# Strassen block products for the input projection of a gated hybrid block, with linear attention's operands kept in DRAM

## The chip, the cores and the metric

One core of one Trainium2 chip runs the whole kernel. The metric is the device time of one execution in microseconds (us). Its compute engines are TensorE (PE, with its weight loads as PEld), VectorE (DVE), ScalarE (ACT) and GpSimd (POOL); SyncE (SP) issues nearly all transfers. Each engine works through its own list of instructions in a fixed order.

## The reference, cut to what matters

One decoder block over 1024 tokens of width 1024, in float32:

```
u  = RMSNorm(h)
z  = u @ W_in                   # 1024 x 1024 @ 1024 x 4272
c_q, c_kv, k_rope, g_q, g_k, g_v, g_lr, g_og, gate_a, gate_b = split(z)
y_a = mla(c_q, c_kv, k_rope, ...) @ W_oA     # softmax attention, 8 heads
y_b = gla(g_q, g_k, g_v, g_lr, g_og, ...) @ W_oB   # gated linear attention, 4 heads, chunked scan
h  = h + (sigmoid(gate_a) * y_a + sigmoid(gate_b) * y_b) @ W_out
h  = h + SwiGLU(RMSNorm(h)); out = RMSNorm(h)
```

The widths of the split are 384, 256, 32, 256, 256, 512, 16, 512, 1024, 1024. `gla` gates each key channel by a decay that depends on the token (`g_lr`), normalises each head's output and multiplies it by `silu(g_og)`.

## The kernel before

Every float32 product is made of three TensorE passes (`mm3`, L122 to L127): each operand is split into a rounded high part and the rest (`hi`, `lo`), and hi*hi, hi*lo and lo*hi are summed in PSUM. `split` (L106) rounds on ScalarE and subtracts on GpSimd.

The kernel runs in stages, all in one function `block_kernel`.

- **Start.** Eight token tiles of x are normalised (`norm_in`), transposed (`transpose_in`) and split into `uh`, `ul`: features on partitions, for each half of 512 tokens 8 chunks of the contraction. The first projections start in between (`begin`).
- **Projection.** `proj` takes 128 columns of W_in, one half of the tokens and 8 chunks: 24 matmuls of 512 columns. `proj_tm` makes token-major results with 256 columns. Queries, keys, values and log gates of linear attention come first and stay in SBUF (`q_fm`, `k_fm`, `b_fm`, `v_tm`); `spill` computes the rest (latents, branch gates) and sends it to DRAM from two staging tiles (`stg`, tag `st`).
- **Linear attention** (L334 to L438). Four units (two token halves, two pairs of heads). The level part of a unit builds the 128 x 128 score blocks `A` by seven levels m = 64 to 1: E = exp of decay differences (DVE L362, ACT L363 and L364), X = E*k (POOL L366), a block-diagonal query `qbd` = E*q (two DVE operations L373), four matmuls (L377) and a masked copy into `A` (DVE L379). The state part goes through four token tiles: output and state update on TensorE (L407 to L414), state (DVE L422, L424), sum of squares (ACT L431), reciprocal root (L87 on DVE, L88 on POOL) and scaling (DVE L437).
- Then the rest of the gates, the latents' norms and up-projections, the softmax attention (scores `pss` from L690), the merge, and a feed-forward part, which uses Strassen products already (`wpair`, `wsums`, `prod`).

The tile scheduler (`schedule_with_timeline_sim=True`) fixes each engine's list when the program is built: it goes by the order of the code, by free tiles and by its own model of time. The engine lists are therefore the same in each run.

Of the kernel before, what the change touches and what calls it, by code (L numbers as in the profile page):

```python
# [10 lines left out]
F32 = mybir.dt.float32  # L11
# [9 lines left out]
P = 128  # L21
# [22 lines left out]
ZFIRST = {29: 0, 31: 1}  # L44

@with_exitstack
def block_kernel(ctx, tc, x, positions, ln_mix, w_in, norm_cq, w_uq, norm_ckv, w_ukv, w_oa,
# [18 lines left out]
    d_c = dram.tile([704, S], F32, name="d_c")  # L66
    d_ob = dram.tile([512, S], F32, name="d_ob")
# [31 lines left out]
    def wraw(n):  # L99
        return wpool.tile([P, D], F32, name="wr", tag="wr", bufs=3)[:, :n]  # L100
# [29 lines left out]
    stg = pool("stg", bufs=2, side="left")  # L130
# [4 lines left out]
    upool = pool("upool", side="left", c=pux)  # L135

# [3 lines left out]
    uh, ul = [], []  # L140
    for h in range(2):
        us = [uslot(h).rearrange("p (e n) -> p e n", e=2) for c in range(KC)]
        uh.append([u[:, 0, :] for u in us])
        ul.append([u[:, 1, :] for u in us])
# [6 lines left out]

    win = w_in[0]

    def proj(hi, lo, half, M=P):
        ps = bank("mm")
        for c in range(KC):
            mm3(ps[:M], hi[:, c, :], lo[:, c, :], uh[half][c], ul[half][c], c == 0, c == KC - 1)
        return ps

    with ExitStack() as s1:  # L160
        xpool = pool("xpool", side="right", c=s1)

        def load_x(t):
            xt = xpool.tile([P, D], F32, name="xt", tag="xt", bufs=4)
            nc.sync.dma_start(xt, x2[t * P:(t + 1) * P, :])
            return xt

        def norm_in(xt):
            ssq = small.tile([P, 1], F32, name="ssq", tag="ssq")
            xs = xpool.tile([P, D], F32, name="xn", tag="xn", bufs=5)  # L170
            nc.scalar.activation(xs, xt, AF.Square, accum_out=ssq)
            r = small.tile([P, 1], F32, name="rx", tag="rx")
            rstd_of(r, ssq, 1, 1.0 / D, small)
            nc.vector.tensor_scalar(xs, xt, r, None, ALU.mult)
            return xs

        def transpose_in(xn, half):
            for c in range(KC):
                ps = bank("mm" if c < 4 and half == 0 else "g")
                for i in range(4):  # L180
                    nc.tensor.transpose(ps[:, i * P:(i + 1) * P], xn[i][:, c * P:(c + 1) * P], ident)
                gc = g_mix[:, c:c + 1]
                nc.scalar.activation(uh[half][c], ps, AF.Copy, scale=gc)
                nc.vector.scalar_tensor_tensor(ul[half][c], ps, gc, uh[half][c].bitcast(F32), ALU.mult,  # L184
                                               ALU.subtract)


        first = []

        def begin(off):  # L190
            w = wload(win[:, off:off + P], KC, P)
            first.append((w, proj(*w, 0)))

        transpose_in([norm_in(load_x(t)) for t in range(4)], 0)
        begin(O_GQ)
        begin(O_GQ + P)
        xn = [norm_in(load_x(t)) for t in range(4, 8)]
        begin(O_GK)
        transpose_in(xn, 1)
        begin(O_GK + P)  # L200
# [17 lines left out]
    wg2 = g.tile([P, HALF], F32, name="wg2", tag="kdT", bufs=1)[0:32, 0:256]  # L218
    nc.sync.dma_start(wg2[0:16, :], w_gate2[0])
    nc.sync.dma_start(wg2[16:17, :], b_gate)  # L220

    def proj_tm(w, t, n=256):
        ps = bank("mm")
        h, o = divmod(t, 4)
        for c in range(KC):
            ts = slice(o * P, (o + 1) * P)
            mm3(ps[:, :n], uh[h][c][:, ts], ul[h][c][:, ts], w[c][0], w[c][1], c == 0, c == KC - 1)
        return ps

    q_fm, k_fm, b_fm = ([[g.tile([P, HALF], F32, name=f"{nm}{p}{h}") for h in range(2)] for p in range(2)]  # L230
                        for nm in ("gq", "gk", "gb"))
    for off, dst, sc in ((O_GQ, q_fm, 0.125), (O_GK, k_fm, 1.0)):
        for p in range(2):
            w, ps = first.pop(0)
            for half in range(2):
                if half:
                    ps = proj(*w, half)
                nc.scalar.activation(dst[p][half], ps, AF.Copy, scale=sc)  # L238


    raw, hi, lo = wtiles(KC * 80)
    v3 = lambda t: t.rearrange("p (c n) -> p c n", c=KC)
    nc.sync.dma_start(v3(raw)[:, :, 0:16], win[:, O_LR:O_LR + 16].rearrange("(c p) n -> p c n", p=P))
    nc.sync.dma_start(v3(raw)[:, :, 16:48], win[:, O_KR:O_KR + 32].rearrange("(c p) n -> p c n", p=P))
    for (a, b) in ((0, 16), (32, 64)):
        o = 0 if a == 0 else 16
        nc.scalar.copy(v3(hi)[:, :, a:b], v3(raw)[:, :, o:o + b - a])
    nc.scalar.copy(v3(hi)[:, :, 64:80], v3(raw)[:, :, 32:48])
    nc.scalar.copy(v3(hi)[:, :, 16:32], v3(raw)[:, :, 16:32])
    for (a, b, o) in ((0, 16, 0), (32, 64, 16), (64, 80, 32), (16, 32, 16)):  # L250
        nc.vector.tensor_tensor(v3(lo)[:, :, a:b], v3(raw)[:, :, o:o + b - a], v3(hi)[:, :, a:b].bitcast(F32),
                                ALU.subtract)
    hi, lo = v3(hi), v3(lo)
    glr = g.tile([32, S], F32, name="glr", tag="A", bufs=2)
    nc.gpsimd.memset(glr, 1.0)
    for half in range(2):
        ps = proj(hi, lo, half, M=80)
        hs = slice(half * HALF, (half + 1) * HALF)
        nc.vector.tensor_copy(glr[0:16, hs], ps[0:16])
        st = stg.tile([P, HALF], F32, name="st", tag="st")  # L260
        nc.scalar.copy(st[0:80], ps[0:80])
        nc.sync.dma_start(d_c[640:672, hs], st[32:64])
        nc.sync.dma_start(d_c[672:688, hs], st[64:80])
        nc.sync.dma_start(d_c[688:704, hs], st[32:48])
# [33 lines left out]
    v_tm = [g.tile([P, 512], F32, name=f"v{t}") for t in range(NT)]  # L298
    for p in range(2):
        w = wload2(win[:, O_GV + p * 256:O_GV + (p + 1) * 256], 256)  # L300
        for t in range(NT):
            ps = proj_tm(w, t)
            nc.any.tensor_copy(v_tm[t][:, p * 256:(p + 1) * 256], ps[:, :256])


    la = []
    for i in range(4):
        ps = bank("g")
        for j in range(2):
            t = 2 * i + j  # L310
            nc.tensor.matmul(ps[:, j * 256:(j + 1) * 256], glr[0:17, t * P:(t + 1) * P], wg2[0:17, :],
                             start=True, stop=True)
# [3 lines left out]
        l = g.tile([P, HALF], F32, name="la", tag="on", bufs=8)  # L316
# [4 lines left out]
    for half in range(2):  # L321
        for p in range(2):
# [6 lines left out]
            nc.vector.tensor_copy(b_fm[p][half], ps)  # L329
# [11 lines left out]
    on = [None] * NT  # L341
    nq = 0
    state = [0, 0]
    for half in range(2):
        for p in range(2):
            q, k, b = q_fm[p][half], k_fm[p][half], b_fm[p][half]
# [51 lines left out]
            kdT = g.tile([P, HALF], F32, name="kdT", tag="kdT", bufs=1)  # L398
            nc.scalar.copy(kdT, psT)
            for i in range(4):  # L400
# [7 lines left out]
                for hd in range(2):  # L408
                    nc.tensor.matmul(po[:, hd * P:(hd + 1) * P], A[:, i * 2 + hd, :],
                                     v_tm[t][:, p * 256 + hd * P:p * 256 + (hd + 1) * P],  # L410
# [15 lines left out]
                if p == 0:  # L426
                    on[t] = g.tile([P, 512], F32, name="on", tag="on", bufs=8)
# [912 lines left out]
```

## Time and profile before

| | us |
|---|---|
| runs | 1539.46, 1539.59, 1542.38 (median 1539.59) |
| profiled execution | 1542.38, span of its instructions 1540.6 |
| PE busy / DVE / ACT / POOL | 1495.2 / 879.6 / 618.2 / 543.1 |
| mean granted TensorE clock | 0.993 of full speed |

The busy time of TensorE is modelled from pipelined matmuls, so 97% busy does not say that it issues at its full rate; the distance from one matmul's start to the next does. `ps_mm` and `ps_g` are the two sets of four PSUM banks that the projection and linear attention use. Where "x4" in the code is shown as "x8" in the trace, a plain float32 matmul runs as two instructions.

### The profile page before, as it was taken

What the parts mean: (1) busy time and instruction counts of PE and PEld (TensorE: products, weight loads), DVE (VectorE), ACT (ScalarE), POOL (GpSimd) and SP (SyncE); (2) the same over time, 40 slices, a digit from 0 to 9 for tenths busy, and PEclk for the clock granted to TensorE, in tenths of its full rate; (3) what the DMA queues carried; (4) which work ended last, traced back from release to release, by engine and by line L of the source; (5) the groups of instructions that cost most, each with busy time, mean ns of one, the idle gap of its engine ahead of it and who ended that gap; (6) DMA issues with size and microseconds to landing.
All of it is one profiled execution on the core that took longest, in us unless ns stands there. A gap on an engine that the chain in (4) does not pass through costs nothing.

```text
span 1540.6 us, 20721 instructions
## 1 busy us (share of the span) xinstructions
PE 1495.2 (97%) x7850; PEld 1255.6 (82%) x7850; DVE 879.6 (57%) x1250; ACT 618.2 (40%) x1217; POOL 543.1 (35%) x444
## 2 busy tenths in 40 slices
PE   7999999999999999999999989999999999799997
PEld 6797888888778888887899868888888888688886
DVE  4125676461412677565632776666666666786785
ACT  5335332333423667566411632222222223254454
POOL 4313353432411223232731355555555555100000
PEclk9999999999999999999999999999999999899999
DMA  7211222213411003346742213333323334943461
GB/s 204 59 52 49 68 67 71 76 35 114 153 56 41 23 21 103 97 137 214 237 165 83 83 41 103 103 103 103 98 96 100 103 103 167 379 134 99 125 210 55
DMA packets 123589, 166.85 MB, mean 108 GB/s; under 512 B 12049, under 2 KB 82210, under 8 KB 123490
## 3 DMA queue, kind: packets, MB, share of 16 engines
q1 hardware_dynamic: 122914, 163.70, 32.7%
q10 hardware_dynamic: 576, 1.84, 0.3%
q8 instruction: 62, 1.02, 0.3%
q14 instruction: 37, 0.30, 0.1%
HBM read 117.80 MB, written 47.71 MB: 107 GB/s over the span
## 4 chain that ended last, share of the span: by engine, by line
PE 83%; DVE 6%; POOL 2%; issue 2%; DMA 2%; ACT 2%; DVEq 0%; ACTq 0%; POOLq 0%; SPq 0%
PE ps_mm L126 7%; PE ps_mm L125 7%; PE ps_mm L127 7%; PE psB L126 6%; PE psB L127 6%; PE psB L125 6%; PE psA L125 5%; PE psD L125 5%; PE psD L126 5%; PE psD L127 5%; PE psA L126 4%; PE psA L127 4%; PE acc L722 2%; PE pspt L713 2%; PE pj L125 2%
## 5 line engine op out<-in xcount | busy, mean ns | idle before, releaser
L125 PE MATMUL ps_mm<-u,wh 128*128 128x512 f32 (+1 forms) x416 | 166.7, 401 | 1.7 <-DVE u L184 0.9
L126 PE MATMUL ps_mm<-u,wh 128*128 128x512 f32 (+1 forms) x416 | 167.0, 402 | 0.0
L127 PE MATMUL ps_mm<-u,wl 128*128 128x512 f32 (+1 forms) x416 | 166.1, 400 | 0.0
L108 POOL TENSOR_TENSOR wl<-wr,wh 128x1024 fp32r<-128x1024 f32 x41 | 100.3, 2452 | 147.0 <-ACT wh L107 128.2
L88 POOL TENSOR_TENSOR rx<-rs_m,nhalf 128x1 f32<-128x1 f32 x24 | 15.1, 637 | 250.8 <-DVE rs_m L87 249.4
L125 PEld LDWEIGHTS ps_mm<-u,wh 128*128 128x128 f32 (+1 forms) x416 | 78.0, 188 | 21.8 <-ACT gq L238 1.2
L942 POOL TENSOR_TENSOR ws<-sS,ws 128x512 fp32r<-128x512 f32 x44 | 70.7, 1616 | 68.7 <-ACT ws L941 68.7
L126 PEld LDWEIGHTS ps_mm<-u,wh 128*128 128x128 f32 (+1 forms) x416 | 77.9, 187 | 19.4 <-issue 1.0
L127 PEld LDWEIGHTS ps_mm<-u,wl 128*128 128x128 f32 (+1 forms) x416 | 78.0, 188 | 18.7 <-issue 0.2
L941 ACT CAST ws<-xr 128x512 fp32r<-128x512 f32 x77 | 47.4, 621 | 90.3 <-PE psB L127 40.0
L107 ACT CAST wh<-wr 128x1024 fp32r<-128x1024 f32 x41 | 43.0, 1048 | 86.0 <-PE ps_mm L126 24.7
L942 DVE TENSOR_TENSOR ws<-xr,ws 128x512 fp32r<-128x512 f32 x77 | 52.8, 688 | 41.2 <-ACT ws L941 35.8
L988 ACT COPY p<-psA 128x512 f32<-128x512 f32 x22 | 12.9, 587 | 157.2 <-PE psA L127 157.2
L125 PE MATMUL ps_mm<-wh,u 128*128 128x256 f32 x256 | 72.3, 282 | 0.0
L127 PE MATMUL ps_mm<-wh,u 128*128 128x256 f32 x256 | 72.2, 282 | 0.0
L126 PE MATMUL ps_mm<-wl,u 128*128 128x256 f32 x256 | 72.2, 282 | 0.0
L126 PE MATMUL psB<-UT,ws 128*128 128x512 f32 x176 | 69.8, 397 | 1.9 <-DVE UT L942 1.9
L125 PE MATMUL psA<-UB,ws 128*128 128x512 f32 x176 | 69.7, 396 | 0.7 <-ACT p L988 0.7
L125 PE MATMUL psB<-UT,ws 128*128 128x512 f32 x176 | 69.8, 396 | 0.1
L127 PE MATMUL psB<-UT,ws 128*128 128x512 f32 x176 | 69.5, 395 | 0.0
L127 PE MATMUL psA<-UB,ws 128*128 128x512 f32 x176 | 69.5, 395 | 0.0
L126 PE MATMUL psA<-UB,ws 128*128 128x512 f32 x176 | 69.3, 394 | 0.0
(408 smaller groups left out, 4423.3 us busy)
## 6 DMA issues: line engine op xcount, KB each, us to landing
xr<-d_a SPq DMA_DIRECT2D x77, 256.0 KB, 2.8
wr<-in_w_in_dram SPq DMA_DIRECT2D x33, 512.0 KB, 3.9
wr<-in_ffn_w_gate_dram SPq DMA_DIRECT2D x22, 512.0 KB, 3.8
wr<-in_ffn_w_up_dram SPq DMA_DIRECT2D x22, 512.0 KB, 3.8
d_a<-p SPq DMA_DIRECT2D x20, 512.0 KB, 2.9
dr<-in_ffn_w_down_dram SPq DMA_DIRECT2D x14, 512.0 KB, 8.0
d_a<-R SPq DMA_DIRECT2D x10, 512.0 KB, 2.6
xt<-in_x_dram SPq DMA_DIRECT2D x8, 512.0 KB, 5.5
```

Source lines behind the costliest of these rows:

```text
L88: nc.gpsimd.tensor_tensor(dst, m, nhalf[:, :n], ALU.pow)
L107: nc.scalar.copy(hi, raw)
L108: (lo_eng or nc.gpsimd).tensor_tensor(lo, raw, hi.bitcast(F32), ALU.subtract)
L125: nc.tensor.matmul(ps, ah, bh, start=first, stop=False, **kw)
L126: nc.tensor.matmul(ps, ah, bl, start=False, stop=False, **kw)
L127: nc.tensor.matmul(ps, al, bh, start=False, stop=last, **kw)
L713: nc.tensor.transpose(ps[:, o * P:(o + 1) * P], pts[i][:, (j0 + jj) * P:(j0 + jj + 1) * P], ident)
L722: nc.tensor.matmul(acc[:, a:256], V[j][:, h, :], src[:, jj * 256:jj * 256 + 256 - a], start=j == 0 and k == 0, stop=j == nj - 1 and k == 1 ...
L941: nc.scalar.copy(dst[:, 0], src)
L942: (lo_eng or nc.gpsimd).tensor_tensor(dst[:, 1], src, dst[:, 0].bitcast(F32), ALU.subtract)
L988: nc.scalar.copy(tt[:, 0:HALF], psA)
```

## The change

The input projection is done by Strassen's scheme in Winograd's form. A pair of 128-column blocks is taken together, and tokens and contraction are each cut in two halves: of the 2 x 2 x 2 block products, 8 before, 7 are made (each 4 chunks, 12 matmuls of 512 columns), with sums of blocks around them. The sums on the side of the activations (`T2`, `T3`, `T1`, `T4` beside the blocks `B11`, `B21`, `B22`) are made and split once at the start; the sums of weights and of results are made for each pair. All splits of this part subtract on VectorE instead of GpSimd. 17 pairs cover the projection (the values of linear attention count as two, token-major). Queries, keys, values and log gates of linear attention go to DRAM (`d_q`, `d_b`, `d_v`) and come back for each unit; its `silu(g_og)` is stored in `d_og` and multiplied in later (`z_second`). `stg` has 5 tiles instead of 2, `wr` 4 instead of 3.

```
+def sp(x):
+    t = wslot().rearrange("p (e c n) -> p e c n", e=2, c=4)
+    split_to(t, x, nc.vector)
+    return t
+def bprod(ps, a, b, first, last):
+    for c in range(4):
+        mm3(ps, a[:, 0, c], a[:, 1, c], T[b][c][:, 0], T[b][c][:, 1], first and c == 0, last and c == 3)
+def p_first(w):
+    w["a"] = bank()
+    bprod(w["a"], sp(w["A11"]), "B11", True, True)
+    w["U2"] = sttile()
+    nc.scalar.copy(w["U2"], w["a"])
+def p_second(w, out):
+    bprod(w["a"], sp(w["A12"]), "B21", False, True)
+    out(0, 0, w["a"], True)
+def p_rest(w, out, opened=False, final=False, pre={}):
+    U2 = w["U2"]
+    plus(w["A21"], w["A21"], w["A22"])
+    minus(w["A11"], w["A21"], w["A11"])
+    psb = bank()
+    bprod(psb, sp(w["A11"]), "T2", True, True)
+    plus(U2, U2, psb)
+    if not opened:
+        p_second(w, out)
+    minus(w["A12"], w["A12"], w["A11"])
+    minus(w["A11"], w["A11"], w["A22"])
...
+    bprod(psc, sp(w["A11"]), "T3", True, True)
+    U3 = sttile()
+    plus(U3, U2, psc)
...
+        bprod(psd, sp(w["A21"]), "T1", True, True)
+        C22 = sttile()
+        plus(C22, U3, psd)
+        out(1, 1, C22, False)
...
+        bprod(pse, sp(w["A22"]), "T4", True, True)
...
+            plus(U3, U3, pse)
+            out(1, 0, U3, False)
...
+    bprod(psd, sp(w["A12"]), "B22", False, True)
+    plus(U2, U2, psd)
+    out(0, 1, U2, False)
+def pair(load, out):
+    w = weights(load)
+    p_first(w)
+    p_rest(w, out)
...
+            p12 = turned(xn, c)
+            nc.vector.scalar_tensor_tensor(T1, p12, g0, raw0[c][:, 0:HALF], ALU.mult, ALU.subtract)
+            p22 = turned(xn, c + 4)
+            nc.vector.scalar_tensor_tensor(T2, p22, g1, T1, ALU.mult, ALU.subtract)
...
+            split_to(T["T2"][c], T2, nc.vector)
...
-            nc.vector.tensor_copy(b_fm[p][half], ps)
+            bt = sttile()
+            nc.vector.tensor_copy(bt, ps)
+            nc.sync.dma_start(d_b[p * P:(p + 1) * P, half * HALF:(half + 1) * HALF], bt)
...
-            q, k, b = q_fm[p][half], k_fm[p][half], b_fm[p][half]
+            q, k, b = (g.tile([P, HALF], F32, name=f"g{nm}", tag=f"g{nm}", bufs=n)
+                       for nm, n in (("q", 2), ("k", 2), ("b", 1)))
+            nc.sync.dma_start(q, d_q[p * P:(p + 1) * P, hs])
...
+            nc.sync.dma_start(b, d_b[p * P:(p + 1) * P, hs])
...
-    spill(O_CKV, 256, d_c, 384)
-    spill(O_CQ, 256, d_c, 0)
...
+    pair(columns(O_CQ), store(d_c, (0, P)))
+    pair(columns(O_CQ + 256), store(d_c, (256, 384)))
+    for i in range(2):
+        pair(columns(O_OG + i * 256), store(d_og, (i * 256, i * 256 + P), AF.Silu))
+    for i in range(3):
+        pair(columns(O_GA + i * 256), store(d_ga, (i * 256, i * 256 + P)))
```

In the code, `pair` stands behind linear attention, as `spill` did. The engine lists show where the scheduler puts it. TensorE in the middle of linear attention, before (L125 to L127 are projection, L377 the level matmuls):

```order
L126 MATMUL ps_mm<-u_98,wh 128x512
L127 MATMUL ps_mm<-u_98,wl 128x512
L125 MATMUL ps_mm<-u_99,wh 128x512
L126 MATMUL ps_mm<-u_99,wh 128x512
L377 MATMUL ps_g<-qbd_1234,X 128x128 x4
L377 MATMUL ps_g<-qbd_1233,X 128x128 x4
L127 MATMUL ps_mm<-u_99,wl 128x512
L125 MATMUL ps_mm<-u_100,wh 128x512
L126 MATMUL ps_mm<-u_100,wh 128x512
L127 MATMUL ps_mm<-u_100,wl 128x512
```

The projection's matmuls stand between those of the levels. TensorE after the change, the end of one unit's level part and the first of its state part (L593 and L613 are the level matmuls and the transposes of the keys, L623 to L630 the state part):

```order
L593 MATMUL ps_g_1451<-qbd0_1379,X_1447 128x128 x4
L593 MATMUL ps_g_1465<-qbd1_1380,X_1461 128x128 x4
L593 MATMUL ps_g_1479<-qbd0_1379,X_1475 128x128 x4
L593 MATMUL ps_g_1493<-qbd1_1380,X_1489 128x128 x4
L593 MATMUL ps_g_1507<-qbd0_1379,X_1503 128x128 x4
L613 MATMUL ps_g_1522<-ident_72,kd_1518 128x128 x4
L625 MATMUL ps_g_1529<-gv_1399,A_1402 128x128 x2
L630 MATMUL ps_g_1529<-gv_1399,kdT_1527 128x256
L623 MATMUL ps_g_1544<-st01_1384,qe_1513 128x256
L625 MATMUL ps_g_1544<-gv_1399,A_1402 128x128 x2
L630 MATMUL ps_g_1544<-gv_1399,kdT_1527 128x256
L623 MATMUL ps_g_1560<-st00_1383,qe_1513 128x256
```

No matmul of the projection stands here any more, nor anywhere between the first level matmul and the last transpose of the fourth unit: of the 12 pairs behind linear attention, four products of the first pair stand ahead of it and all else behind.

ScalarE after the change, at the end of the fourth unit (L644 squares, L657 the unit's result to a staging tile; L203 is the copy in `p_first`, L274 the one in `store`, L159 the rounding in `split_to`):

```order
L644 ACTIVATE on_2044,ssq2_2195<-ps_g_2188 128x128 x2
L644 ACTIVATE on_2044,ssq2_2211<-ps_g_2204 128x128 x2
L644 ACTIVATE on_2044,ssq2_2224<-ps_g_2220 128x128 x2
L657 ACTIVATE st_2238<-ps_g_2233,g_gn_1391 128x512
L657 ACTIVATE st_2246<-ps_g_2241,g_gn_1391 128x512
L203 COPY st_2269<-ps_mm_2253 128x512
L274 ACTIVATE st_2305<-ps_mm_2253 128x512
L159 CAST ws_2481<-wr_2383 128x512
L159 CAST ws_2498<-wr_2383 128x512
L203 COPY st_2402<-ps_mm_2386 128x512
```

The copy of the first pair's first product into its staging tile `U2` stands directly behind the last staging tile that linear attention fills; on VectorE the first `plus(U2, U2, psb)` follows in the same way behind the last scaling of the fourth unit.

VectorE after the change at the start (L333 and L335 make `T1` and `T2` from transposed tokens, L160 subtracts in a split, L176 is `minus`, L338 splits `B22`; `v4` tiles hold `T2` and `T3`, `k4` those of `T4`):

```order
L333 SCALAR_TENSOR_TENSOR t12_391<-ps_g_392,g_mix_79,raw0_113 128x512
L160 TENSOR_TENSOR v4_322<-t12_374,v4_322 128x512
L160 TENSOR_TENSOR k4_337<-raw0_111,k4_337 128x512
L160 TENSOR_TENSOR k4_338<-raw0_112,k4_338 128x512
L335 SCALAR_TENSOR_TENSOR t12_391<-ps_g_398,g_mix_79,t12_391 128x512
L176 TENSOR_TENSOR raw0_113<-raw0_113,t12_391 128x512 x2
L338 SCALAR_TENSOR_TENSOR u1_331<-ps_g_398,g_mix_79,u1_331 128x512
L160 TENSOR_TENSOR v4_323<-t12_391,v4_323 128x512
L160 TENSOR_TENSOR v4_324<-raw0_110,v4_324 128x512
```

The last row here completes `T2`; it is the 72nd VectorE instruction of the program, and the first product that uses `T2` as a whole waits for it. Before, VectorE had 8 splits of `ul` behind the first four norms.

## Rows read from the trace of the kernel before

**Rows 1.** the page, part 1, whole span: busy us (share of the span) xinstructions
```profile
PE 1495.2 (97%) x7850; PEld 1255.6 (82%) x7850; DVE 879.6 (57%) x1250; ACT 618.2 (40%) x1217; POOL 543.1 (35%) x444
```

**Rows 2.** TensorE one by one, 146 to 151 us: start us, us, engine, line, operation
```profile
146.05 0.39 PE L126 MATMUL ps_mm<-u,wh 128*128 128x512 f32 x1
...
150.71 0.40 PE L125 MATMUL ps_mm<-u,wh 128*128 128x512 f32 x1
```

**Rows 3.** the same view, 119 to 131 us, the 256-column matmuls
```profile
119.93 0.28 PE L125 MATMUL ps_mm<-wh,u 128*128 128x256 f32 x1
...
121.57 0.27 PE L127 MATMUL ps_mm<-wh,u 128*128 128x256 f32 x1
```

**Rows 4.** the same view, the matmuls of L311 and those after them
```profile
121.77 3.72 PE L311 MATMUL ps_g<-wg,glr 17*128 17x256 f32 x16
...
126.46 0.63 PE L126 MATMUL ps_mm<-u,wh 128*128 128x512 f32 x1
...
128.59 0.63 PE L125 MATMUL ps_mm<-u,wh 128*128 128x512 f32 x1
```

**Rows 5.** stretches of 20 us, writers of ps_mm alone: busy us (x instructions), granted clock
```profile
core 0: us, PE busy (x) PEld busy (x) DVE busy (x) ACT busy (x), PEclk, DMA share, GB/s
140.00:160.00 20.00, 13.61 (x55) 9.78 (x54) 0.00 (x0) 0.58 (x1) 1.00 0.14 40
```

**Rows 6.** VectorE and TensorE in order of time, first 16 us
```profile
12.19 0.75 DVE L174 TENSOR_SCALAR xn<-xt,rx 128x1024 f32<-128x1024 f32 x1 [0.66 <-POOL rx L88]
...
14.90 2.73 DVE L184 SCALAR_TENSOR_TENSOR u<-ps_mm,g_mix,u 128x512 fp32r<-128x512 f32 x4 [1.97 <-DMA g_gn<-in_gla_norm_dram]
15.71 0.50 PE L125 MATMUL ps_mm<-u,wh 128*128 128x512 f32 x1 [0.91 <-DVE u L184]
```

**Rows 7.** VectorE groups by shape, 1200 to 1540 us: busy us, mean ns
```profile
L942 DVE TENSOR_TENSOR ws<-xr,ws 128x512 fp32r<-128x512 f32 x77 | 52.8, 688 | 41.2 <-ACT ws L941 35.8 <-DMA xr<-d_a 5.4
```

**Rows 8.** VectorE in order of time: first level operation and last norm of linear attention
```profile
137.25 1.29 DVE L362 TENSOR_TENSOR E<-gb 128x512 f32<-128x512 f32 x2
...
343.85 0.61 DVE L437 TENSOR_SCALAR on<-ps_g,rs 128x128 f32<-128x128 f32 x2 [0.81 <-POOL rs L88]
```

**Rows 9.** DMA issues: size, median us from issue to landing
```profile
k<-d_gb SPq DMA_DIRECT2D x16, 256.0 KB, 2.7
...
d_c<-st SPq DMA_DIRECT2D x10, 256.0 KB, 2.0
```

**Rows 10.** VectorE, the last unit of linear attention, level part, 298 to 322 us
```profile
298.62 0.69 DVE L362 TENSOR_TENSOR E<-gb 128x512 f32<-128x512 f32 x1 [2.15 <-PE ps_g L407]
...
307.02 1.87 DVE L373 TENSOR_TENSOR qbd<-E,gq 64x256 f32<-64x256 f32 x2
...
317.04 0.71 DVE L379 COPY_PREDICATED A<-lmask,ps_g 128x512 f32<-128x512 int32 x1
317.64 0.84 DVE L373 TENSOR_TENSOR qbd<-E,gq 64x256 f32<-64x256 f32 x2
...
320.25 1.29 DVE L379 COPY_PREDICATED A<-lmask,ps_g 128x512 f32<-128x512 int32 x1
```

**Rows 11.** VectorE, one token tile of the state part, 187 to 191 us
```profile
187.64 0.72 DVE L424 SCALAR_TENSOR_TENSOR st<-st,ebl,ps_g 64x128 f32<-64x128 f32 x2 [3.37 <-PE ps_g L414]
189.12 0.17 DVE L87 TENSOR_SCALAR rs_m<-ssq 128x2 f32<-128x2 f32 x1 [0.75 <-ACT on L431]
190.10 0.61 DVE L437 TENSOR_SCALAR on<-ps_g,rs 128x128 f32<-128x128 f32 x2 [0.81 <-POOL rs L88]
```

**Rows 12.** TensorE groups of the latents and the rotary key
```profile
L550 PE MATMUL ps_g<-v,ones 128*128 128x512 f32 x8 | 3.8, 602 | 0.2 <-DVE v L545 0.2
...
L538 PE MATMUL ps_g<-ones,v 128*128 128x1 f32 x32 | 3.7, 245 | 0.0
...
L595 PE MATMUL ps_g<-wr,sel 64*128 64x512 f32 x4 | 2.2, 641 | 0.0
```

**Rows 13.** TensorE, the first score matmul of the attention
```profile
504.95 0.22 PE L125 MATMUL pss<-u,u 128*128 128x128 f32 x1
```

More of the change, by code (lines that the diff above doesn't have):

```diff
@@ L44 @@
 ZFIRST = {29: 0, 31: 1}
+STB = 5
+C2B = 22
 @with_exitstack
@@ L150, in bank, with sttile @@
         return ps1.tile([P, 512], F32, name=f"ps_{tag}", tag=tag)
+    def sttile():
+        return stg.tile([P, HALF], F32, name="st", tag="st")
     win = w_in[0]
[L154 to L158, printed above, removed]
+    plus = lambda d, x, y: nc.vector.tensor_tensor(d, x, y, ALU.add)
+    minus = lambda d, x, y: nc.vector.tensor_tensor(d, x, y, ALU.subtract)
@@ new lines, in pair, with store, out @@
+    def pair(load, out):
+        w = weights(load)
+        p_first(w)
+        p_rest(w, out)
+    def store(dst, rows, func=None, scale=1.0):
+        def out(e, half, src, psum):
+            t = src
+            if psum:
+                t = sttile()
+            if psum or func is not None or scale != 1.0:
+                nc.scalar.activation(t, src, func or AF.Copy, scale=scale)
+            nc.sync.dma_start(dst[rows[e]:rows[e] + P, half * HALF:(half + 1) * HALF], t)
+        return out
@@ L177, in transpose_in @@
[L177 to L185, printed above, removed]
@@ L188, in block_kernel, with turned @@
[L188 to L200, printed above, removed]
+            nc.vector.tensor_scalar(xt, xt, r, None, ALU.mult)
+            return xt
+        def turned(xn, c):
+            ps = bank("g")
+            for i in range(4):
+                nc.tensor.transpose(ps[:, i * P:(i + 1) * P], xn[i][:, c * P:(c + 1) * P], ident)
+            return ps
@@ L230, in block_kernel @@
[L230 to L255, printed above, removed]
-    for half in range(2):
-        ps = proj(hi, lo, half, M=80)
-        hs = slice(half * HALF, (half + 1) * HALF)
[L259 to L264, printed above, removed]
+    glr = [g.tile([32, HALF], F32, name="glr", tag="X", bufs=2) for half in range(2)]
@@ L549, in token_rows @@
             ps = bank("g")
-            nc.tensor.matmul(ps, ones, dg[:, half * 4:half * 4 + 4, :], start=True, stop=True)
+            nc.tensor.matmul(ps, ones, dg, start=True, stop=True)
             res.append(ps)
         return res
-    rs_kv, raws = latents(384, 2, "ck")
+    *raws, rs_kv = latents(384, 2, "ck", None)
     ckh, ckl = ck_t
```

412 lines of the change are left out of this document (273 added, 139 removed).

## The prediction

> **What bounds the kernel now.** I read the page first, then the projection's matmuls one by one, then VectorE and TensorE in linear attention. TensorE is busy for 97% of the span [rows 1], and where the projection runs undisturbed it issues at a steady pace: 20 matmuls of 512 columns in 4.66 us, 0.233 us each [rows 2], and 14 of 256 columns in 1.64 us, 0.117 us each [rows 3]. So a matmul left out is worth its 0.233 us as long as TensorE has other work to go on with. Linear attention is where that is in question. It lasts from 137.25 us, the first level operation, to 344.5 us, the last scaling [rows 8], some 207 us, and it is a chain from VectorE over ScalarE and GpSimd to TensorE and back. Its own matmuls are small. TensorE is not idle meanwhile, because the projection is laid between them: 55 of its matmuls in the 20 us from 140 to 160 us [rows 5], 12.8 us of the 20 at 0.233. That cover is what the reader should look at, for the change moves it.
>
> **What is taken away.** 17 pairs make 7 products of 12 matmuls where 8 were made: 17 x 12 = 204 matmuls of 512 columns or as much in 256, 204 x 0.233 = 47.5 us of TensorE. Were all else equal, this would be the gain.
>
> **What is added.** A pair brings 7 splits and 9 sums to VectorE, 16 operations of 0.69 us [rows 7], 11 us beside 84 x 0.233 = 19.6 us of TensorE. In the projection alone TensorE covers that, and ScalarE's and GpSimd's shares are smaller; I cost it at nothing there. The transfers of q, k, v and the gates go beside other work except one, that of the decay sums `b`, which stands in the chain. The multiplication by the stored gate (8 VectorE operations in the attention) is covered likewise. What is left are two places where the engine lists have lost their cover, and I time the new program along them up to the first score matmul, which before starts at 505 us [rows 13]; behind it the lists are nearly the same.
>
> *Start.* The product with `T2` needs 72 VectorE instructions done. The first eight, norms of four token tiles, end at 12.94 us as before [rows 6]. The 64 behind them are 4 scalings of 0.75 us and 20 operations from PSUM of 0.68 us [rows 6], 36 of 0.69 us [rows 7] and 4 small ones of 0.17 us [rows 11]: 3.0 + 13.6 + 24.8 + 0.7 = 42.1 us, so 55 us if VectorE never waits. TensorE has only 48 projection matmuls (11 us) and the transposes until then, where it began its steady run at 15.7 us before [rows 6]; it waits for VectorE some 25 us. Then 204 matmuls of 512 and 336 of 256 columns, to the end of the values: 47.5 + 39.3 = 87 us, to 142 us.
>
> *From the log gates to the first level.* Before, this took from 121.77 [rows 4] to 137.25 us [rows 8], 15.5 us. The sums now go to DRAM and back: a write of 256 KB takes 2.0 us, a read 2.7 us [rows 9], in all 20 us, to 162 us. TensorE's four ready products (11 us) lie inside.
>
> *Linear attention.* No projection matmul is left in it, so its own length counts. The level part of the last unit is the best measure, as VectorE is hardly idle in it: 298.62 to 321.54 us, 22.9 us [rows 10]. It holds one E and one norm more than the new list has (0.69 + 0.17 + 0.61), so 21.4 us; the first unit makes four E and two `qbd` pairs more, at 0.69 and on average 1.36 us (0.84 alone, 1.87 beside GpSimd's X) [rows 10], 27 us. A token tile of the state part takes 187.64 to 190.71 us, 3.1 us, of which 1.56 us are waits for ScalarE and GpSimd [rows 11]; the 3.37 us of waiting for TensorE ahead of it go, since they were the projection's. Four tiles are 12.3 us. Four E and two pairs of the next unit stand in between; they need 5.5 us and fill 3.1 us of waits, 2.4 us more. At a unit's boundary VectorE waits until `b` is loaded again, as it has one buffer: 2.7 us [rows 9] less the masked copy of 0.71 us [rows 10], while the decayed keys go over four engines. Rows bound the boundary by these 2 us from below and from above by 6.4 us, a whole token tile with the wait for TensorE that it had before, 3.07 + 3.37 [rows 11]; I take 4 us, between them. So 27 + 3 x (12.3 + 2.4 + 4) + 3 x 21.4 + (12.3 + 4) = 164 us. The floor is VectorE's own work without a wait: 28 E at 0.69, 28 pairs at 0.84, 28 masked copies at 0.71, 16 tiles at 1.50 and 16 others at 0.69 make 98 us; the ceiling is the 207 us of before [rows 8]. I take 164 us, as all its parts have rows. It ends at 326 us.
>
> *The rest.* Two us for the last transposes and the staging copy that the first pair waits for. Then 1038 matmuls at 0.233 us, 242 us, and 10 us for the latents' and the rotary key's small ones [rows 12]. The first matmuls behind a quiet stretch run slower: after those of L311 five starts lie 2.13 us apart, 0.43 us each [rows 4], so 2 us more. The first score matmul starts at 326 + 2 + 242 + 10 + 2 = 582 us instead of 505 us.
>
> **The sum.** +77 us: about 25 in the start, some 95 of uncovered linear attention and 5 of DRAM, less the 47.5 us of matmuls. The profiled execution took 1542.38 us, span 1540.6 us, and the median of the runs is 1539.59 us, 2.8 us below it; I set the 77 us, rounded down to 76, on the median: **1616 us**. A measurement of this kernel tells 0.2% (3 us) from no change.
>
> **The clock.** After TensorE's sparse matmuls of L311 the next ones ran at 0.43 instead of 0.233 us [rows 4], the lower of its two levels (1.2 and 2.4 GHz). In the sum I let linear attention's small matmuls run as in the rows, because they were hidden behind the longer wait for the projection. The Trainium skill (TensorE: Matmul & The Clock Gate, "What's actually happening") says that a TensorE that has been idle is clocked at 1.2 GHz and one that has been busy at 2.4 GHz; by it all of linear attention would run at the lower level, and where its matmuls stand in the chain that comes out as the second rival.
>
> **The rivals.**
> 1. *Linear attention is much shorter than its parts* (chance 0.18). If E and `qbd` run without GpSimd beside them (POOL has lost the splits and keeps X alone) and the waits fill, it takes 110 to 130 us; 120 makes 1616 - 44 = 1572 us. For it: the floor is 98 us. Against it: the 1.87 us pairs come with X alone.
> 2. *TensorE at the lower clock lengthens the chain* (0.15). A `qbd` pair is followed by four level matmuls, 8 instructions, and a state tile by 8 more; priced like the narrow ones of [rows 3], 0.117 us each, a group takes 0.9 us and at half speed 1.8. If half of the 44 groups stand in the chain, that is 20 us, if all, 40: 1636 to 1656 us. Against it: VectorE has the E of another level to do meanwhile.
> 3. *The pairs do not run at TensorE's pace* (0.06). Each product ends in a VectorE sum, and staging tiles are four to a pair of five, freed 2.0 us after issue [rows 9]. If TensorE waited 2 us in each of the 12 pairs, 24 us: 1640 us.
> 4. *Faster* (0.04): TensorE keeps its cover, and the 47.5 us arrive whole, 1492 us. The place is linear attention: it would have to leave no more idle time than before. With my other terms the point is 87 us from the first level operation to the end (164 - 77); below it the change gains. Against it stand the floor of 98 us and the lists, in which no engine can pass a waiting instruction.
>
> That the change doesn't do what it says I exclude: the lists have 12 matmuls per product and 84 per pair.
>
> **How the numbers follow.** My forecast, linear attention at 135 to 185 us, has 0.57. The range takes it in with the lower half of rival 2 and most of rival 1: 1572 to 1650 us. Slower by over 0.2%: 0.95; within 0.2%: 0.01; faster: 0.04.
>
> **What would show it.** In the profile after: TensorE idle until some 55 us, released by VectorE; no ps_mm matmul between about 162 and 326 us; VectorE with few gaps there; then matmuls 0.233 us apart until about 580 us; the feed-forward part as before, only later. The prediction is wrong if projection matmuls do stand between the level matmuls, if linear attention is far from 164 us, or if time is lost behind 582 us.

## The result and the profile after

| | before | after |
|---|---|---|
| median of the runs | 1540.99 us (4 runs, 1539.46 to 1542.55) | 1652.66 us (4 runs, 1647.37 to 1655.14) |
| profiled execution, its span | 1542.38, 1540.6 us | 1650.85, 1649.1 us |

The ratio is 1.072, with an interval of 1.0688 to 1.0752: slower, as forecast, by 112 us instead of 76, and 2.7 us above the top of the range. All times below are medians; one execution, of run 11, took 2421.19 us at a mean granted clock of 0.557 and is left out of its median. The page of the kernel after, part 1 (busy us, share of the span), answers to [rows 1]: TensorE's share falls from 97 to 92%, VectorE's rises from 57 to 64%.

```profile
PE 1511.1 (92%) x7430; PEld 1251.7 (76%) x7430; DVE 1049.9 (64%) x1539; ACT 666.9 (40%) x1299; POOL 455.6 (28%) x406
```

Stretches of 20 us of the kernel after (us of the stretch, busy us and instructions of each engine, granted clock, DMA share, GB/s) show three holes beside linear attention itself, and between them the pairs at full pace:

```profile
core 0: us, PE busy (x) PEld busy (x) DVE busy (x) ACT busy (x) POOL busy (x), PEclk, DMA share, GB/s
40.00:60.00 20.00, 11.87 (x31) 7.36 (x32) 19.96 (x32) 10.42 (x19) 0.99 (x3) 0.50 0.13 40
160.00:180.00 20.00, 4.46 (x16) 3.63 (x16) 7.61 (x13) 19.49 (x24) 0.00 (x0) 0.58 0.21 66
360.00:380.00 20.00, 20.00 (x87) 16.10 (x86) 10.45 (x17) 5.17 (x9) 0.00 (x0) 1.00 0.49 153
500.00:520.00 20.00, 9.29 (x37) 7.22 (x36) 14.46 (x23) 12.10 (x19) 0.24 (x1) 0.69 0.26 79
```

From 40 to 60 us VectorE is busy throughout (19.96 of 20 us) and TensorE waits for it. The kernel before had this stretch, in the same columns, as follows:

```profile
40.00:60.00 20.00, 19.23 (x88) 15.36 (x87) 4.51 (x9) 7.55 (x16) 8.12 (x17) 1.00 0.16 42
```

The last split of `T2` in the kernel after is this one, to be held against the predicted 55 us:

```profile
57.66 0.68 DVE L160 TENSOR_TENSOR v<-t,v 128x512 fp32r<-128x512 f32 x1
```

From 160 to 180 us it is ScalarE that has hardly a gap (19.49 us), and TensorE does little (4.46 us). ScalarE in order of time shows why: Abs (L518), Exp (L519) and Ln (L525) of the log gates stand between Sin (L503, L507) and Abs (L504) of the rotary table. Each Sin, Exp or Ln behind another of these three has a table load of 1.28 us ahead of it, an Abs has none. There are 11 loads from 154.56 to 181 us, 14 us together; the kernel before has four in its log gates, and made the table from 90 to 96 us, beside the values' matmuls.

```profile
154.56 1.28 ACT L503 ACT_TABLE_LOAD   x1
156.00 0.73 ACT L503 ACTIVATE rot<-ang,fcol 128x512 f32<-128x512 f32 x1 [0.16 <-DVE ang L502]
...
157.28 0.60 ACT L518 ACTIVATE lab<-ps_g 128x512 f32<-128x512 f32 x1
...
158.41 1.28 ACT L519 ACT_TABLE_LOAD   x1
159.70 0.63 ACT L519 ACTIVATE lab<-lab 128x512 f32<-128x512 f32 x1
160.35 1.28 ACT L507 ACT_TABLE_LOAD   x1
161.64 1.27 ACT L507 ACTIVATE rot<-kk 32x512 f32<-32x512 f32 x2
162.93 1.28 ACT L525 ACT_TABLE_LOAD   x1
```

The log gates' first matmul and, in the kernel before, their first Abs (L314 there) are needed for the account below:

```profile
143.97 2.83 PE L515 MATMUL ps_g<-wg,glr 17*128 17x256 f32 x12
```

```profile
123.10 0.60 ACT L314 ACTIVATE lab<-ps_g 128x512 f32<-128x512 f32 x1
```

VectorE then waits 6.41 us for the last two Ln, and the first level operation starts at 183.26 us, where 162 was forecast and the kernel before had 137.25 [rows 8]:

```profile
182.04 1.29 DVE L526 TENSOR_TENSOR la<-la,lab 128x512 f32<-128x512 f32 x2 [6.41 <-ACT lab L525]
183.26 1.29 DVE L578 TENSOR_TENSOR E<-gb 128x512 f32<-128x512 f32 x2
```

The Trainium skill (ScalarE: Activation LUTs, "Table sets: the hidden batching unit") says to group calls by table set. The trace agrees that going back and forth costs loads, 11 instead of 4; it differs on two points, and decides: a load takes 1.28 us here where the section states about 2.7, and there is a load between Exp and Ln too, for which the section names a common set.

Linear attention ends at TensorE with the last transposes, which start at 340.81 us. The pair behind it then waits for ScalarE's copy of its first product into its staging tile (L203):

```profile
340.81 0.59 PE L655 MATMUL ps_g<-ident,on 128*128 128x128 f32 x2 [0.91 <-DVE on L649]
342.98 0.50 PE L131 MATMUL ps_mm<-u,ws 128*128 128x512 f32 x1 [1.57 <-ACT st L203]
```

From 347 us on the pairs' matmuls start 0.233 us apart, as forecast, until some 502 us. There the latents' small matmuls come, and TensorE in order of time has two waits, 10.7 us, before it goes on at 519.34 us. L721 sums the squares of the query latents, L175 is `plus`:

```profile
504.67 0.40 PE L133 MATMUL ps_mm<-u,ws 128*128 128x512 f32 x1
509.81 1.84 PE L721 MATMUL ps_g<-ones,st 128*128 128x1 f32 x8 [4.74 <-DVE st L175]
517.62 1.86 PE L721 MATMUL ps_g<-ones,st 128*128 128x1 f32 x8 [5.98 <-DVE st L175]
519.34 0.77 PE L131 MATMUL ps_mm<-u,ws 128*128 128x512 f32 x1
```

The first score matmul starts at 611.1 us (504.95 before [rows 13]). Behind it the two kernels take 1038.0 and 1035.6 us, so all but 2.4 us was lost ahead of it.

### The profile page after: what moved, and what is told of

Its sections match the earlier page's. It is cut to its first block, busy times and chain, and to the rows that moved or that the text cites. A ratio compares the mean times of both kernels' runs of the same rounds, so it can differ in the third digit from the quotient of the medians.

```text
span 1649.1 us, 20435 instructions
## 1 busy us (share of the span) xinstructions
PE 1511.1 (92%) x7430; PEld 1251.7 (76%) x7430; DVE 1049.9 (64%) x1539; ACT 666.9 (40%) x1299; POOL 455.6 (28%) x406
## 5 line engine op out<-in xcount | busy, mean ns | idle before, releaser
L159 ACT CAST ws<-wr 128x512 fp32r<-128x512 f32 x171 | 103.2, 619 | 149.9 <-PE ps_mm L133 111.3
L160 DVE TENSOR_TENSOR ws<-wr,ws 128x512 fp32r<-128x512 f32 x149 | 133.9, 912 | 24.5 <-ACT ws L159 23.5
L175 DVE TENSOR_TENSOR st<-st,ps_mm 128x512 f32<-128x512 f32 x85 | 58.1, 685 | 72.0 <-PE ps_mm L133 67.3
L131 PE MATMUL ps_mm<-u,ws 128*128 128x512 f32 x240 | 98.5, 411 | 2.5 <-ACT st L203 1.6
L132 PE MATMUL ps_mm<-u,ws 128*128 128x512 f32 x240 | 98.0, 408 | 1.1 <-DVE u L313 1.0
L133 PE MATMUL ps_mm<-u,ws 128*128 128x512 f32 x240 | 96.2, 408 | 0.0
L160 POOL TENSOR_TENSOR ws<-sS,ws 128x512 fp32r<-128x512 f32 x44 | 70.6, 1614 | 68.1 <-ACT ws L159 68.1
L159 ACT CAST ws<-xr 128x512 fp32r<-128x512 f32 x77 | 47.3, 621 | 86.6 <-PE psB L133 38.8
L160 DVE TENSOR_TENSOR ws<-xr,ws 128x512 fp32r<-128x512 f32 x77 | 52.7, 688 | 38.1 <-ACT ws L159 34.1
L593 PE MATMUL ps_g<-qbd,X 128*128 128x128 f32 x224 | 46.5, 386 | 26.9 <-DVE qbd L589 26.5
L582 POOL TENSOR_TENSOR X<-E,gk 128x512 f32<-128x512 f32 x28 | 38.9, 1399 | 97.3 <-ACT E L580 79.0
L593 PEld LDWEIGHTS ps_g<-qbd,X 128*128 128x128 f32 x224 | 42.3, 287 | 30.6 <-POOL X L582 25.6
L900 DVE TENSOR_TENSOR ws<-pspt,ws 128x512 fp32r<-128x512 f32 (+1 forms) x80 | 49.5, 631 | 19.3 <-ACT ws L899 18.9
L131 PEld LDWEIGHTS ps_mm<-u,ws 128*128 128x128 f32 x240 | 46.6, 194 | 15.2 <-ACT u L312 1.8
```

The source lines that it names most:

```text
L131: nc.tensor.matmul(ps, ah, bh, start=first, stop=False, **kw)
L132: nc.tensor.matmul(ps, ah, bl, start=False, stop=False, **kw)
L133: nc.tensor.matmul(ps, al, bh, start=False, stop=last, **kw)
L159: nc.scalar.copy(dst[:, 0], src)
L160: (lo_eng or nc.gpsimd).tensor_tensor(dst[:, 1], src, dst[:, 0].bitcast(F32), ALU.subtract)
L175: plus = lambda d, x, y: nc.vector.tensor_tensor(d, x, y, ALU.add)
```

## The experiments

In all of them the times of the kernel before, on the same chips, had medians of 1540.85 to 1541.13 us. Where no profile line is shown, starts are those of the first level operation (E, L578) and of the first score matmul in that run's trace.

**1. The ring.** The pairs and linear attention's eight output tiles share one ring of five staging tiles (`st`). A pair's first tile comes behind those eight in the program.

```
-                st = sttile()
+                st = g.tile([P, HALF], F32, name="st", tag="X", bufs=2)
                 nc.scalar.activation(st, psT, AF.Copy, scale=g_gn)
```

> Linear attention's eight output tiles leave the ring of five staging tiles that the pairs use; nothing else. Theory A (the ring alone kept the pairs behind linear attention): projection matmuls stand between the level matmuls again. From the first level operation at 183 us there are 242 us of projection matmuls at 0.233 us and some 73 us of other matmuls up to the first score (what was left in 137 to 505 us of the kernel before: 368 us less 1048 x 0.233 and 384 x 0.117 and 6 idle), so the first score comes at 500 to 525 us instead of 611, and the time falls by 86 to 111 us, to 1540 to 1567 us. Theory B (VectorE, with 16 operations of a pair added between the level operations, is the bound of the mixed stretch): linear attention stretches past 260 us and no more than 50 us come back, 1600 us or more.

Measured: 1594.72 us, ratio 1.0347 (1.0331 to 1.0364), 58 us less than after. The cover is back: from 200 us on TensorE has about 100 instructions in 20 us at full clock. The stretches (columns as above) show where the forecast gain stops:

```profile
200.00:220.00 20.00, 20.00 (x111) 16.96 (x110) 19.80 (x30) 8.24 (x18) 5.59 (x4) 1.00 0.37 119
...
400.00:420.00 20.00, 12.82 (x71) 11.28 (x69) 19.17 (x28) 5.01 (x12) 7.87 (x6) 0.76 0.10 26
420.00:440.00 20.00, 9.65 (x44) 6.92 (x43) 6.53 (x20) 4.64 (x20) 4.58 (x8) 0.84 0.17 50
440.00:460.00 20.00, 8.90 (x28) 6.26 (x28) 10.92 (x18) 8.21 (x14) 1.64 (x1) 0.50 0.23 77
```

With cover, linear attention lasts until 435 us, but the pairs ahead of the latents run out soon after 400, and the first score comes at 558.5 us. So theory A holds for the ring, and its number does not: it left out that cover can end early. Theory B holds in part: linear attention takes 251 us (184.8 to 435.4) instead of 158, near its 260, with VectorE busy for 19.80 of 20 us in the first stretch shown. Pairs and levels share VectorE, so here cover made the covered chain longer.

**2. The rotary table.** In the kernel after, its code stands behind the values, and its positions and `kk` take buffers of tag X, of which both hold the gates' low-rank input `glr` until L515 has read it; so the table can't start before that. The log gates' `lab` in turn shares tag E with the table's `ang`; their first Abs comes at 157.28 us, behind the table's first Sin and Abs, though L515 began at 143.97 us. The edit puts the values behind the table and gives the table staging tiles.

```
-    values_gla()
-
     frow = stg.tile([P, HALF], F32, name="st", tag="st")[0:1, 0:2 * P].rearrange("p (a b) -> p a b", a=2)
...
-        pos_i = g.tile([P, HALF], I32, name="pos_i", tag="X", bufs=2)
+        pos_i = sttile().bitcast(I32)
-        kk = g.tile([P, HALF], F32, name="kk", tag="X", bufs=2)
+        kk = sttile()
...
+    values_gla()
+
     la = []
```

> The rotary table is built ahead of the values, with staging tiles for its positions, so that it no longer waits for the log gates' buffers; the rest as changed. Theory A (the rotary's Sin and Abs and their table loads between the log gates' Exp and Ln delayed the first level operation): first level operation 14 to 22 us earlier, at 161 to 169 us instead of 183, time 1631 to 1639 us. Theory B (the log gates' own chain and the trip through DRAM are the length): at most 6 us earlier, 1647 us or more.

Measured: 1637.97 us, ratio 1.0626 (1.0605 to 1.0648). The first level operation comes 17.6 us earlier (this run's E group: count, shortest, median and longest ns, first and last start), the first score 11.0 us earlier, as linear attention itself took 164 instead of 158 us. In runs 1, 3, 5, 6 and 12, whose edits don't touch this part, that operation came at 184.8 to 189.2 us.

```profile
L578 DVE TENSOR_TENSOR E<-gb x28: 667/692/694, 165.7 to 306.0; 128x512 f32<-128x512 f32 x28
```

These are theory A's numbers, so the place of the table was the cause. What theory A says of the table loads is not shown by this run. In its trace the table's Sin (L504 here) still stands between the gates' Exp and Ln, with ten loads from 113 to 143 us, but all of it now runs beside the values' matmuls, which last until 152.8 us. The last thing that VectorE waits for ahead of the first level operation is now the transfer of `b`:

```profile
130.50 1.28 ACT L504 ACT_TABLE_LOAD   x1
131.79 1.27 ACT L504 ACTIVATE rot<-st 32x512 f32<-32x512 f32 x2
```

```profile
165.68 1.29 DVE L578 TENSOR_TENSOR E<-gb 128x512 f32<-128x512 f32 x2 [0.49 <-DMA gb<-d_b]
```

**3. The latents in weight-load tiles.**

```
-                raw = sttile() if n == 3 else c2(F32)
+                two = wraw(S) if n == 3 else None
+                raw = two[:, 0:HALF] if n == 3 else c2(F32)
-                s_ = sttile()
+                s_ = two[:, HALF:S] if n == 3 else sttile()
```

> The query latents' rows and their squares come in weight-load tiles instead of staging tiles. Theory A (the staging ring makes TensorE wait from 505 to 519 us): the wait goes for the most part, 8 to 14 us less, 1639 to 1645 us. Theory B (the chain from ScalarE's squares over VectorE's sums is the length whatever holds the rows): less than 4 us, 1649 us or more.

Measured: 1653.94 us, ratio 1.0737 (1.0717 to 1.0757), no gain. That is theory B's time, but TensorE's wait had only changed its tile: six rows now queue for four weight-load tiles, which the pairs use too. L722 sums the squares here; the second view is that of the transfer queue, whose load of a row (L712) waited 11.4 us until a tile came free (L754).

```profile
506.62 1.71 PE L722 MATMUL ps_g<-ones,wr 128*128 128x1 f32 x8
518.52 1.86 PE L722 MATMUL ps_g<-ones,wr 128*128 128x1 f32 x8 [10.20 <-DVE wr L175]
```

```profile
SPq L712 <- DVE c L754: 11.6, 2, 11.4
```

**4. The three edits together.**

> The edits of the three runs before this one together. If all three are right and independent: 1652.7 - 98 - 18 - 11 = 1526 us, between 1505 and 1550, so below the kernel before (1541 us). If with cover restored the rotary table and the latents are hidden anyway, they add little and it stays at the time of the first run, about 1553 us.

Measured: 1580.67 us, ratio 1.0261 (1.0236 to 1.0285), outside what was expected if all were independent, and 14 us below run 1, about what the table gave alone (15 us). The first score comes at 546.3 us; between 360 and 445 us TensorE again lacks pairs, at a granted clock of 0.5 to 0.82 in its stretches of 20 us. Earlier pairs leave fewer for later.

**5. The start.**

```
-                split_to(T["T3"][c], T3, nc.vector)
+                split_to(T["T3"][c], T3, nc.gpsimd)
...
```

(The same for T4, three of T2's four tiles and the first four weight tiles.)

> At the start GpSimd instead of VectorE makes the low halves of the first two pairs' first weights, of three of the four T2 tiles and of T3 and T4; the rest as changed. Theory A (VectorE's list alone sets when T2 is ready): some 15 of its operations before T2's last split leave, 0.6 us of issue each, so T2 is ready at 47 to 51 us instead of 58 and the time falls by 7 to 11 us, to 1642 to 1646 us. Theory B (its waits for ScalarE and for x, some 17 us in the first 58, only grow): less than 3 us, 1650 us or more.

Measured: 1657.34 us, ratio 1.0733 (1.0705 to 1.0762), no gain. Ten operations, not 15, left VectorE ahead of `T2`'s last split, which still ended at 59.0 us (58.3 after). VectorE's groups in the first 62 us (busy us, mean ns, idle before) say why; first the kernel after:

```profile
L176 DVE TENSOR_TENSOR raw<-raw,t 128x512 f32<-128x512 f32 x8 | 5.2, 681 | 0.0
...
L333 DVE SCALAR_TENSOR_TENSOR t<-ps_g,g_mix,raw 128x512 f32<-128x512 f32 x4 | 2.9, 740 | 0.0
```

then this run (L335 here is L333 there):

```profile
L176 DVE TENSOR_TENSOR raw<-raw,t 128x512 f32<-128x512 f32 x8 | 9.4, 1210 | 0.0
...
L335 DVE SCALAR_TENSOR_TENSOR t<-ps_g,g_mix,raw 128x512 f32<-128x512 f32 x4 | 3.0, 742 | 0.8 <-PE ps_g L300 0.8
```

With GpSimd at work on tiles of SBUF, VectorE's sums of two SBUF tiles take 1210 instead of 681 ns, while those that read PSUM stay at 742 (740 after). Within this run, the pair of them that started at 51.46 us, while GpSimd was idle (50.68 to 52.18 us), took the usual time, and the next pair, beside GpSimd's splits, 3.35 us:

```profile
51.46 1.28 DVE L176 TENSOR_TENSOR raw<-raw,t 128x512 f32<-128x512 f32 x2
...
53.98 3.35 DVE L176 TENSOR_TENSOR raw<-raw,t 128x512 f32<-128x512 f32 x2
```

What left the list came back in the price of what stayed. So theory A had the number of operations and their durations wrong, and theory B, whose time it is, had the reason wrong: VectorE's waits did not grow (16.1 us in the first 62 us of the kernel after, 14.8 us here).

**6. The latents in tiles with a free slot.** Rows, squares and diagonals use the half tiles `c2`; a square stands in the tile that its latent's high half fills later.

```
-                raw = sttile() if n == 3 else c2(F32)
+        raw = c2(F32)
-                s_ = sttile()
+            cr = squares(0, half, c, cqh[half][0], cqh[half][c])
...
-            dg = sttile().rearrange("p (t n) -> p t n", t=4)
+            dg = c2(F32).rearrange("p (t n) -> p t n", t=4)
```

> The latents' rows and squares and the diagonals use tiles of the attention's own ring of half tiles, with more than one slot free, and neither staging tiles nor weight-load tiles. Theory A (the wait at 505 to 519 us comes from sharing a ring with the pairs, first the staging ring and, in the run with the weight-load tiles, that one): pairs' matmuls now stand between the latents' small ones, and 10 to 15 us come back, 1638 to 1643 us. Theory B (the latents' chain over ScalarE and VectorE is itself what TensorE waits for): less than 4 us, 1649 us or more.

Measured: 1635.43 us, ratio 1.0631 (1.0573 to 1.0688); the interval is wide because one of the four runs took 1653.62 us, so the trace carries the reading. From linear attention's end (345.1 us) to the first score (599.6 us) there are 254.5 us instead of 270. That is theory A, and run 3 is explained. The stretch that had 9.29 us of TensorE is full:

```profile
500.00:520.00 20.00, 20.00 (x84) 15.51 (x83) 15.18 (x24) 11.13 (x18) 0.00 (x0) 1.00 0.32 94
```

**7. Cover everywhere.** Runs 1, 2 and 6 together, and

```
+    for i in range(3):
+        pair(columns(O_GB + i * 256), store(d_gb, (i * 256, i * 256 + P), AF.Sigmoid))
...
-    for i in range(3):
-        pair(columns(O_GB + i * 256), store(d_gb, (i * 256, i * 256 + P), AF.Sigmoid))
```

> Own tiles for linear attention's outputs, the rotary table ahead of the values, the latents as in the run before this one, and three pairs of the second gate ahead of the latents. In the run with three edits together TensorE lost, at the lower clock or idle, 40 to 50 us between 360 and 445 us, where its projection matmuls had run out before the end of linear attention and the latents. Theory A (cover, wherever it is missing, is what is lost): 35 to 45 us less than that run, 1536 to 1546 us, as fast as the kernel before (1541 us). Theory B (linear attention's own chain then stretches by as much as it is covered, VectorE being shared with the pairs): 1560 us or more.

Measured: 1543.07 us, ratio 1.0005 (0.9992 to 1.0017), the time of the kernel before: theory A. The first score comes at 504.5 us. What is left of waiting at TensorE is the start, some small gaps, and one hole behind the last pair:

```profile
480.00:500.00 20.00, 10.43 (x31) 5.20 (x31) 13.25 (x22) 11.53 (x20) 3.04 (x3) 0.77 0.00 0
```

**8. The same with the start of run 5.**

> The run before this one and the splits at the start on GpSimd. If the two are independent, 7 to 11 us less than the run before, some 1532 us, and below the kernel before (1541 us); if the end of linear attention, not the start of the projection, sets the first score, no change against the run before.

Measured: 1543.35 us, ratio 1.0008 (0.9995 to 1.002): no change, as the start itself had not become shorter.

**9 and 10. Two ways at the last hole.** Run 9 leaves the third of these three pairs behind the latents and loads the query latents into staging tiles; run 10 drops run 6 from run 7.

> As the run with everything covered, but only two pairs of the second gate ahead of the latents, the third behind them, and the query latents' rows in staging tiles. In that run TensorE still waits or runs slowly from 480 to 504 us, behind its last pair: some 25 us for work worth 11. Theory A (one more pair there hides the query latents' chain): the first score comes 10 to 14 us earlier, near 492 us, and the time falls to 1528 to 1534 us, 0.5 to 0.8% below the kernel before. Theory B (linear attention's end, not the order of the pairs, sets the latents, and the uncovered time moves to linear attention's last unit): within 4 us of that run, 1539 to 1545 us.

> Only three edits of place against the changed kernel: own tiles for linear attention's outputs, the rotary table ahead of the values, and three pairs of the second gate ahead of the latents, whose tiles are as changed. Theory A (behind the pairs the latents' chain no longer shares its ring with anybody, and the pairs' order does the rest): as the run with everything covered or better, 1531 to 1543 us. Theory B (the latents need tiles of their own): the wait of 505 to 519 us of the changed kernel is back, 1550 us or more.

Measured: run 9 1555.92 us, ratio 1.0097 (1.0081 to 1.0112); run 10 1542.65 us, ratio 1.0008 (0.9999 to 1.0018). In run 9 the hole is earlier, from the last pair ahead of the latents (439 us) to the third pair (467.66 us), and larger, a case that neither theory had:

```profile
440.00:460.00 20.00, 7.89 (x22) 4.94 (x22) 8.62 (x16) 5.19 (x9) 3.40 (x4) 0.59 0.23 79
```

Run 10 has theory A's time, but not its reason. TensorE's two waits of the kernel after, 4.74 and 5.98 us, are there again:

```profile
463.41 1.84 PE L721 MATMUL ps_g<-ones,st 128*128 128x1 f32 x8 [4.48 <-DVE st L175]
470.85 1.87 PE L721 MATMUL ps_g<-ones,st 128*128 128x1 f32 x8 [5.59 <-DVE st L175]
```

They cost no more than run 7's hole, and the first score comes at 504.5 us in both. So own tiles for the latents, worth 15 us by themselves in run 6, are worth nothing on top of the other edits.

**11. The last hole again.** As run 7, with the query latents' rows in staging tiles.

> As the run with everything covered, all three pairs of the second gate ahead of the latents, but the query latents' six rows in staging tiles, so that they are loaded without waiting for two free slots. Theory A (the query latents came late for want of slots, and TensorE's wait at 480 to 504 us is theirs): their small matmuls come some 10 us earlier and 5 to 12 us come back, 1531 to 1538 us, below the kernel before (1541 us). Theory B (the chain from linear attention's end at 431 us over the latents to the first score is as long anyway): 1540 to 1546 us.

Measured: 1547.56 us, ratio 1.0042 (1.0029 to 1.0055), above both forecasts and no better than run 7. There is no trace of an execution of this length, so only the time stands, and why it lost 4.5 us is open.

**12. The clock in linear attention.**

```
+                spare = bank()
+                for i in range(2):
+                    nc.tensor.matmul(spare, ident, X, start=i == 0, stop=i == 1)
```

> The changed kernel with two spare matmuls of 512 columns on X beside each of the 28 level groups, whose result nobody reads (the output is the same). They run while TensorE waits for qbd. Theory A (TensorE's lower clock in linear attention lengthens its chain): the granted clock there rises from 0.5 to 0.74 towards 1, the level matmuls fall from a mean of 386 towards 278 ns, and linear attention gets 8 to 20 us shorter than 158 us, 1633 to 1645 us. Theory B (VectorE and its waits for ScalarE and GpSimd make the chain): linear attention 155 to 165 us as before, 1649 to 1660 us, whatever the clock does.

Measured: 1656.71 us, ratio 1.0752 (1.0734 to 1.077). TensorE's level group, from 183 to 343 us after:

```profile
L593 PE MATMUL ps_g<-qbd,X 128*128 128x128 f32 x224 | 46.5, 386 | 26.9 <-DVE qbd L589 26.5 <-DVE A L570 0.4
```

and in this run, from 180 to 350 us (L597 are the spare matmuls):

```profile
L597 PE MATMUL ps_mm<-X,ident 128*128 128x512 f32 x112 | 57.4, 638 | 8.5 <-POOL X L582 8.5
L593 PE MATMUL ps_g<-qbd,X 128*128 128x128 f32 x224 | 30.6, 283 | 1.6 <-DVE qbd L589 1.6
```

The granted clock rose to 0.80 to 1.00, the level matmuls fell from 386 to 283 ns, and linear attention took 165 us (186.4 to 351.4) instead of 158. That is theory B's time. The test is not a clean one: the spare matmuls hold TensorE for 57.4 us of this stretch themselves and could have eaten a gain of some us. How much VectorE could have gained is bounded by its waits for TensorE in the kernel after, 183 to 342 us (total us, times, longest):

```profile
DVE A L595 <- PE ps_g L593: 8.6, 11, 1.6
DVE st L640 <- PE ps_g L630: 7.6, 7, 3.0
```

With 2.5 us more for the diagonal blocks (L570) they make 18.7 of the 158 us; the rest of the chain is VectorE's own work and its waits for ScalarE, GpSimd and transfers. By the Trainium skill's rule that the prediction cites (TensorE: Matmul & The Clock Gate, "What's actually happening") the uncovered stretch had to run at the lower level. Its rows agree in part: the granted clock of the kernel after was 0.50 to 0.91 in the stretches of 20 us from 180 to 340 us.

## Why the prediction was right and wrong

The direction and the cause were right: a gain of matmuls, a long start, and linear attention without cover. By its own steps, against the profiled execution:

| step | forecast | measured |
|---|---|---|
| T2 ready | 55 us | 58.3 us |
| end of the values | 142 us | 144 us |
| from there to the first level operation | 20 us | 39 us |
| linear attention | 164 us | 158 us |
| from its end to the first score | 256 us | 270 us |
| behind the first score | 0 | +2.4 us |

*The start* came within 3 us, since VectorE's list bounds it; that it came so close is partly luck. The sum let VectorE never wait, and it waited 6.4 us between 12.9 and 58.3 us; and it priced operations at their durations of 0.68 to 0.75 us, while those of the trace start 0.60 to 0.66 us apart, which gave 3 us back. *Linear attention* was summed from parts to within 6 us, and no projection matmul stood in it.

**The step that failed** is "From the log gates to the first level": to the 15.5 us of before it added a write and a read of DRAM and nothing else, 20 us, and it took 39. DRAM was not the reason, and cost nothing here: the load of `b` was issued at 176.55 us and took 2.6 us, while VectorE waited for Ln until 182.04 us. But the change had also put the rotary table's code behind the values and given `glr` both buffers of tag X, so the table, which the kernel before had finished by then, came between the log gates. The two traces show where the 24 us beyond 15.5 went. From the gates' first matmul to their first Abs there are 13.3 us instead of 1.3, as they waited for the table's buffers. From that Abs to the first level operation there are 26.0 us instead of 14.2, with eleven table loads instead of four and the table's own functions in between. Run 2, which brings the table and with it the log gates back beside the values' matmuls, gives back 17.6 us; as it keeps ten loads, no run shows what the loads alone cost. For this stretch the prediction read only VectorE's and TensorE's lists, and the new neighbours stand in ScalarE's.

The second is "The rest": the latents were priced by their TensorE rows alone [rows 12], 10 us, as if cover went with them. Their waits of 10.7 us are most of the 14 us in the table; run 6 takes the hole away, and the term comes to 254.5 us, where 256 was forecast. The two terms, 19 and 14 us, less the 6 us of linear attention, with 2 us each at the values and behind the first score, make 31 of the 32 us between the profiled execution and its forecast (1616 + 2.8 us).

*The rivals.* The lower clock lengthening the chain would have given the right time for the wrong reason: its 1636 to 1656 us hold the result. But it needs linear attention 20 to 40 us longer than forecast, and linear attention was 6 us shorter, so it wasn't that. Nor was linear attention much shorter (158 us, not 110 to 130). Pairs did run at TensorE's pace, 87 matmuls in 20 us. Faster, with cover kept, did not come; run 7 shows that cover, with the table and the latents in their places, is worth 110 us here, and that even then the 47.5 us of matmuls only pay for what else the change brings. In run 7 most of the time of the matmuls left out is spent again in three places ahead of the first score. In the first 60 us TensorE is busy 36.6 us, against 49.8 us before, a third of that at half clock; from 480 to 504.5 us it needs 25 us for work worth some 11; and gaps from 160 to 440 us sum to 9 us, against 4 us before. By an estimate from these figures that is 13 + 6 + 14 + 5 = 38 of the 47.5 us; where the rest went is open.

No run's median came out below that of the kernel before. Whether a shorter start would do it was not settled, as run 5 did not make it shorter.

## What to carry to other kernels

Work that is to cover a chain must be able to get ahead of it: look at which ring of buffers each of its tiles comes from, and who stands before it in that ring, not only at dependences of data. When a buffer is given a new, longer tenant, list what else used that buffer, for that work will be moved to another place, on engines that the edit never names. And closing one hole in a list moves the next one: count what work is left for cover behind the last one.

## What was not expected of the hardware

GpSimd beside VectorE slowed VectorE's sums of two SBUF operands from 681 to 1210 ns (run 5), while those with a PSUM operand took 740 and 742 ns. The Trainium skill (SBUF — State Buffer, "Who interferes with whom") says that a VectorE instruction with two SBUF inputs contends with a GpSimd instruction that reads SBUF; the trace agrees. What that costs is this run's own figure: the splits moved to GpSimd cost VectorE about what they relieved it of.

TensorE's level matmuls of 128 columns took 283 ns instead of 386 when spare work kept the granted clock up, and the kernel did not get faster (1656.71 against 1652.66 us): in this stretch TensorE mostly waited for others, and a lower clock that falls into such waits costs little.
